# A hybrid attention block on Trainium2: a least distance between the score rows of four attention units in a build-time schedule

## The chip, the core and the metric

The kernel runs on one core of a Trainium2 chip. The metric is the time of one execution on the device, in microseconds (us). The kernel before takes 422.29 us, the median of three runs (421.83 to 422.44).

## The reference

One decoder layer with two token mixers on an input of 512 tokens and 1024 channels in fp32. Both read one normed input through one combined projection. The first mixer ("A", MoBA) has eight heads of 64 channels with block-sparse attention. The sequence has only two blocks of 256 keys and the top three are taken, so every query sees all keys before it. The second mixer ("B", NSA) has eight heads with a compressed, a selected and a window branch. Both outputs are gated, projected and merged, and go through one output projection. What matters here is the attention of mixer A:

```python
def moba_mixer(q, k, v, bias_tab):
    scale = 1.0 / math.sqrt(Dh)
    ...
    def one_chunk(c):
        ...
        logits = jnp.einsum('bhqd,bhqnkd->bhqnk', qc, kg).astype(jnp.float32) * scale
        dist = tq[:, None, None] - (sc[..., None] * MOBA_BLOCK + offs)
        bias = bias_tab[hi[..., None], t5_bucket(dist)]
        logits = jnp.where(dist >= 0, logits + bias, NEG)
        p = jax.nn.softmax(logits.reshape(B, H, Q_CHUNK, -1), axis=-1).astype(v.dtype)
        return jnp.einsum('bhqm,bhqmd->bhqd', p, vg.reshape(B, H, Q_CHUNK, -1, Dh))
...
    h = rms_norm(x, norm_w[l])
    proj = h @ w_in[l]
    ...
    k_cmp = rms_norm(compress(heads(kc), cmp_pos_k[l], cmp_w1_k[l], cmp_w2_k[l]), k_norm_cmp[l])
    ...
    merged = g_m[..., :D_MODEL] * (y_a @ w_branch_a[l]) + g_m[..., D_MODEL:] * (y_b @ w_branch_b[l])
    x = x + merged @ w_out[l]
```

## The kernel before

**Tiling.** Tokens come in four tiles of 128 rows. fp32 products are made of three passes over a high and a low part: L402 casts a weight tile to its high part on ScalarE (ACT), L412 subtracts it on VectorE (DVE) for the low part, and L437 holds the three matmuls. The projections go one group of columns after another (`ORDER`: `qk0 v kc vc qk1 za0 kb za1 za2 qb za3 vb zb0` and so on); then come the gates and branch products of both mixers and the output product, in the same stream (`gemms`).

**The attention.** A *unit* is one head of mixer A (units 0 to 7) or one head and branch of mixer B (units 8 to 23). Units 0 to 3 use the queries and keys of the group `qk0`, units 4 to 7 those of `qk1`. A unit has four *rows*, one for each 128 queries, and takes the longest first (512, 384, 256, 128 keys). For each row:

- `Unit.qk` (L1078) takes one of the two PSUM banks for scores (`room("s")`, L1085) and makes two matmuls into `sps` (L1094).
- `bias` (L1107) adds the bias table `T` and takes the row's minimum on DVE (L1114). That reads the bank out and frees it. The result goes to a buffer `sb`.
- `soft` (L1121) takes the exponential with its sum on ACT (L1125), scales by the reciprocal (L1127, L1128) to a high half in fp16 on ACT (L1132) and makes the low half on DVE (L1136).
- `send` (L1057) transposes both halves by DMA into `dst` (L245, on the SP queue).

A `Pair` takes two units; `pv` (L1157) makes their value products `O` (L1168) when all eight rows are in `dst`. Units 4 and 5 are one pair, 6 and 7 the next. The bias table of a unit is fetched by `load_bias` (L887) into one of two buffers. The outputs of mixer A are wanted by the branch products (`branch`, L1383), which come behind all projections.

**The compression** (`compress_h`, L930) runs beside: its weights `in_w` are loaded and split (`vh`, `vl`, by L402 and L412 as well), multiplied into `hps` (L940), copied to `hs` by ACT (L947) and transposed by the small product `pu` (L952).

**What sets the order.** Nothing on the chip decides an order: the program is laid out while it is built, and each engine then takes its instructions in that order. The build walks a clock `now` in ns, from costs that it is given for each kind of work. The work on TensorE (PE) comes from streams, one generator each: scores, gemms, compression, values and others. A stream that yields a number has put that much work on PE; one that yields a function waits until the function gives a time that has passed. The loop takes, among the streams that are ready by their *margin*, the one with the least share used so far:

```python
        ws = [(r, r.wait()) for r in live]
        ok = ([r for r, w in ws if w is not None and w + r.margin <= now[0]] or
              [r for r, w in sorted(((r, w) for r, w in ws if w is not None and w <= now[0]), key=lambda z: z[1])[:1]])
```

The margin of the scores is `LATE_A` = 1000, of the values `LATE_V` = 2000, of the compression `LATE_C` = 300, of the gemms `MARGIN` = 300. The work of DVE, ACT and GpSimd comes as a `Chain` of steps behind a matmul; a step is put in its engine's order when the step before it is done by the costs (`Chain.step`, L203). Loads and transposes are put in the SP queue's order in the same way (`dma`, L236; `dma_transpose`, L243). `scores` (L1339) goes through the units in order and through each unit's rows.

Of the kernel before, what the change touches and what calls it, by code (L numbers as in the profile page):

```python
# [58 lines left out]
SHARE_C = 100.0  # L59
LAG = 20000  # L60
MARGIN = 300
LATE_A = 1000
LATE_V = 2000
LATE_S = 1000
# [44 lines left out]
def hybrid_kernel(ctx: ExitStack, tc: tile.TileContext, x, x0, xT, wtok, wchan, gains, w1,  # L109
# [21 lines left out]
    now = [0.0]  # L131
# [41 lines left out]
    class Chain:  # L173


        def __init__(c, t=None, held=False):
            c.t = now[0] if t is None else t
            c.q = deque()
            c.held = held
# [370 lines left out]
    def x_rms():  # L550
        yield need("sq")
        ready = done["sq"] + XW
        yield lambda: ready
        yield room("o")
        ps = psum("o", "pss")
        for t in range(NT):
            nc.tensor.matmul(ps[:, t:t + 1], sq_sum[:, t * P:(t + 1) * P], ones, start=True, stop=True)
            yield 214
            if t < NT - 1:
                ready = now[0] + XG  # L560
                yield lambda: ready
        c = Chain(now[0] + 230)
        c.do({"D": 70}, lambda e: e.tensor_scalar(rx, ps[:, :NT], 1.0 / D, EPS, op0=ALU.mult, op1=ALU.add), ps)
        c.do({"p": 1030}, lambda e: e.tensor_tensor(rx, rx, mhalf[:, :NT], op=ALU.pow))
        c.mark("rx").call(lambda: [fn() for fn in rx_todo])
        x_diag(c)
# [188 lines left out]
    def qk_used(*keys):  # L755
        for k in keys:
            qkt[k]["uses"] -= 1
            if not qkt[k]["uses"]:
                release(qkt[k]["t"])
# [573 lines left out]
    def prepare():  # L1333
        for n, (pre, _) in enumerate(units):
            yield lambda: 0.0 if n <= begun[0] + 2 else None
            yield from pre()
            prepared.add(n)

    def scores():  # L1339
        for n, (_, u) in enumerate(units):  # L1340
            yield lambda: 0.0 if n in prepared else None
            begun[0] = n
            for b in reversed(range(NT)):
                yield from u.qk(b)
            qk_used(u.q[:2], u.ks[:2])

# [4 lines left out]
    def values():  # L1351
        for p in pairs:
            yield from p.pv()
            todo_units[0] -= 2
# [272 lines left out]
    def cmp():  # L1627
        yield from compress_h(0)
        yield from compress_h(1)


    class Run:
        def __init__(r, gen, share, margin=MARGIN):
            r.gen, r.share, r.vt, r.wait, r.live, r.margin = gen, share, 0.0, lambda: 0.0, True, margin
# [10 lines left out]
    for k in range(KT):  # L1645
        x_split(k)
        x_square(k)
    load_consts()
    now[0] = 3500.0
    A, F, C, X, B, V = Run(scores(), SHARE_A, LATE_A), Run(gemms(), SHARE_F), Run(cmp(), SHARE_C, LATE_C), Run(x_rms(), 100.0), Run(prepare(), SHARE_B), Run(  # L1650
        values(), SHARE_V, LATE_V)
    Z = Run(starts(), 100.0)
# [95 lines left out]
```

## Time and profile before

| | |
|---|---|
| median of three runs | 422.29 us |
| the profiled execution | 422.54 us |
| its span, first to last instruction | 420.5 us |
| PE busy, matmuls | 411.8 us |
| DVE busy | 356.3 us |
| ACT busy | 297.9 us |
| the DMA queue's packets | 70.5% of 16 engines' span |
| score rows of units 4 to 7, first and last | 112.96 and 149.63 us |

A profile is of one execution. Its lines give an engine, a line of the kernel, an operation and what it writes and reads by the program's names (`out<-in`). Busy time of PE is modelled, since matmuls overlap; idle time between matmuls is what counts. A wait line says who waited for whom: total us, times, longest. A timeline line has the start, the length and, in brackets, the idle time before it and what ended that. Windows give busy time in a stretch of the span. SPq is the queue that issues the DMAs.

### The profile page before, as it was taken

To read this page: it belongs to the slowest core of one execution; us is meant where nothing else is said; L and a number is where in the kernel's file an instruction comes from. 1 tells how busy PE (TensorE), PEld (TensorE's weight loads), DVE (VectorE), ACT (ScalarE), POOL (GpSimd) and SP (SyncE) were. 2 spreads that over 40 slices of the span, in tenths; PEclk is the share of its full clock that TensorE was granted. 3 is DMA by queue.
4 is the path that set the end of the run, shared out by engine and by line. 5 is a ranking of instruction groups with operands and counts; after the bars stand their busy time and mean duration, and the time that the engine had idled before them with its cause. 6 is when DMAs were issued, how large, how long until landed. Compare 5 with 4: busy or idle time off the path is not lost.

```text
span 420.5 us, 7307 instructions
## 1 busy us (share of the span) xinstructions
PE 411.8 (98%) x2235; PEld 322.0 (77%) x2235; DVE 356.3 (85%) x933; ACT 297.9 (71%) x793; POOL 35.1 (8%) x37
## 2 busy tenths in 40 slices
PE   9999998999998999999999999999999999999996
PEld 7877875778976677897766777666777888888885
DVE  5967969999899987778999997899956967698993
ACT  7996748997797988727988897898943433445620
POOL 0015100123210033200000000000000000000000
PEclk9999999999999999999999999999999999999999
DMA  8951785688969988750878778889799597251232
GB/s 278 311 190 49 129 271 140 137 183 214 264 201 232 195 163 194 218 153 12 147 168 196 150 161 200 167 195 160 145 162 348 175 374 278 79 180 44 56 143 100
DMA packets 116693, 75.30 MB, mean 179 GB/s; under 512 B 89072, under 2 KB 92016, under 8 KB 116656
## 3 DMA queue, kind: packets, MB, share of 16 engines
q1 hardware_dynamic: 116656, 74.86, 70.5%
q8 instruction: 17, 0.28, 0.3%
q14 instruction: 20, 0.16, 0.1%
HBM read 51.11 MB, written 2.75 MB: 128 GB/s over the span
## 4 chain that ended last, share of the span: by engine, by line
PE 54%; DVE 23%; DMA 9%; ACT 5%; issue 5%; SPq 1%; POOL 1%; DVEq 0%; ACTq 0%; POOLq 0%
PE pgc L437 21%; PE pbr L437 9%; PE po L437 9%; PE pgt L437 8%; DMA wr<-in_wtok 5%; DVE sb L1114 4%; DVE wl L412 4%; DVE sb L1136 4%; DMA wr<-in_w 3%; PE O L1168 3%; PE sps L1094 3%; ACT wh L402 2%; DVE vl L412 1%; SPq L238 1%; DMA T<-rtab 1%
## 5 line engine op out<-in xcount | busy, mean ns | idle before, releaser
L437 PE MATMUL pgc<-hh,wh 128*128 128x512 f32 x208 | 87.1, 419 | 0.0
L412 DVE TENSOR_TENSOR wl<-wr,wh 128x512 fp32r<-128x512 f32 (+1 forms) x112 | 73.1, 669 | 11.8 <-ACT wh L402 11.6
L437 PE MATMUL pgc<-hh,wl 128*128 128x512 f32 x208 | 81.5, 392 | 0.0
L437 PE MATMUL pgc<-hl,wh 128*128 128x512 f32 x208 | 81.2, 390 | 0.0
L402 ACT CAST wh<-wr 128x512 fp32r<-128x512 f32 (+1 forms) x111 | 64.0, 599 | 11.2 <-DMA wr<-in_wtok 5.6
L1125 ACT ACTIVATE sb<-sb,sst 128x256 f32<-128x256 f32 (+3 forms) x96 | 53.2, 554 | 10.5 <-DVE sst L1114 10.2
L437 PE MATMUL pgt<-wh,hh 128*128 128x512 f32 (+2 forms) x160 | 58.3, 364 | 0.1
L437 PE MATMUL pgt<-wl,hh 128*128 128x512 f32 (+2 forms) x160 | 56.1, 351 | 0.5 <-DVE wl L412 0.4
L437 PE MATMUL pgt<-wh,hl 128*128 128x512 f32 (+2 forms) x160 | 55.8, 349 | 0.0
L1136 DVE SCALAR_TENSOR_TENSOR sb<-sb,sst 128x256 f16<-128x256 f32 (+3 forms) x96 | 51.1, 542 | 4.2 <-ACT sb L1132 3.9
L1114 DVE CUSTOM_DVE_ANT_0 sb<-sps,T,gst 128x512 f32<-128x512 f32 (+3 forms) x96 | 51.2, 541 | 3.5 <-PE sps L1094 1.6
L1132 ACT ACTIVATE sb<-sb,sst 128x256 f16<-128x256 f32 (+3 forms) x96 | 51.4, 552 | 4.0 <-DVE sst L1128 3.7
L437 PEld LDWEIGHTS pgc<-hh,wh 128*128 128x128 f32 x208 | 39.1, 188 | 8.6 <-issue 0.3
L437 PEld LDWEIGHTS pgc<-hh,wl 128*128 128x128 f32 x208 | 39.0, 188 | 8.6
L437 PEld LDWEIGHTS pgc<-hl,wh 128*128 128x128 f32 x208 | 39.2, 189 | 6.5
L1094 PE MATMUL sps<-qkt,qkt 128*128 128x512 f16 (+3 forms) x176 | 38.2, 310 | 1.6 <-DVE sst L1114 1.4
L489 POOL TENSOR_TENSOR nr<-nss,mhalf 128x8 f32<-128x8 f32 (+1 forms) x16 | 29.0, 1819 | 109.4 <-DVE nss L488 47.9
L437 PEld LDWEIGHTS pgt<-wl,hh 128*128 128x128 f32 x160 | 30.1, 188 | 5.5 <-DVE wl L412 1.6
L437 PEld LDWEIGHTS pgt<-wh,hh 128*128 128x128 f32 x160 | 30.2, 189 | 4.3 <-DVE X L912 0.4
L437 PEld LDWEIGHTS pgt<-wh,hl 128*128 128x128 f32 x160 | 30.2, 189 | 3.4
L1094 PEld LDWEIGHTS <-qkt 128*128 128x128 f16 x176 | 11.5, 98 | 21.4 <-issue 18.5
L437 PE MATMUL pbr<-yh,wh 128*128 128x512 f32 x64 | 26.4, 413 | 0.0
(229 smaller groups left out, 746.3 us busy)
## 6 DMA issues: line engine op xcount, KB each, us to landing
wr<-in_wchan SPq DMA_DIRECT2D x52, 256.0 KB, 3.8
wr<-in_wtok SPq DMA_DIRECT2D x36, 256.0 KB, 4.0
wq<-in_wout SPq DMA_DIRECT2D x36, 256.0 KB, 3.1
T<-rtab SPq DMA_DIRECT2D x16, 256.0 KB, 4.0
wr<-in_w SPq DMA_DIRECT2D x16, 256.0 KB, 3.7
wr<-in_wbr SPq DMA_DIRECT2D x16, 256.0 KB, 3.1
xr<-in_x SPq DMA_DIRECT2D x8, 256.0 KB, 5.3
x<-in_xT SPq DMA_DIRECT2D x7, 256.0 KB, 5.8
```

The lines of the kernel that those rows point to most:

```text
L238: nc.sync.dma_start(out=dst, in_=src)
L402: e.copy(hi, raw)
L412: c.do(either(n), lambda e, hi=hi, lo=lo, raw=raw: e.tensor_sub(lo, raw, hi.bitcast(F32))).mark((w, 1, i))
L437: nc.tensor.matmul(dst, sts[i][a], mvs[i][b], start=(start and i == a == b == 0), stop=(stop and i == n - 1 and (a, b) == passes[-1]), ski ...
L489: c.do({"p": 700 + 150 * w}, lambda e: e.tensor_tensor(v(dst), v(ss), mhalf[:parts, :w], op=ALU.pow))
L1094: nc.tensor.matmul(sps[:, :n].rearrange("p (t n) -> p t n", n=P), qs, k4[:, x, j, :b + 1], start=not x, stop=bool(x))
L1114: e.tensor_tensor_reduce(z["sb"], sps[:, :L], T[:, S - L:], scale=nrunscale, scalar=3e38, op0=ALU.add, op1=ALU.min, accum_out=st[:, 0, b:b ...
L1125: c.do({"A": 279 + 0.834 * L}, lambda e: e.activation(z["sb"], z["sb"], AF.Exp, bias=st[:, 0, b:b + 1], scale=-1.0, accum_out=st[:, 1, b:b ...
L1132: e.activation(z["pp"][:, :L], z["sb"], AF.Copy, scale=s_)
L1136: c.do({"d": 59 + cd(L)}, lambda e: e.scalar_tensor_tensor(z["pp"][:, L:], z["sb"], s_, z["pp"][:, :L], op0=ALU.mult, op1=ALU.subtract))
L1168: nc.tensor.matmul(out, v[r][kb][:, vi * DH:(vi + 1) * DH], u.moving(kb, pi), start=p.first and kb == vi == pi == 0, stop=p.last and kb == ...
```

## The change

The stream of scores gets a least distance. For units 4 to 7 it remembers the earliest time of the last row, `beat`; before each row it sets `beat` to the later of the clock and the old `beat` plus 2500 ns, and waits for that time before `qk`, which then waits for its keys and a free bank as before. All other units are as they were.

```diff
+BEAT = 2500
...
+    beat = [0.0]
+
     def scores():
         for n, (_, u) in enumerate(units):
             yield lambda: 0.0 if n in prepared else None
             begun[0] = n
             for b in reversed(range(NT)):
+                if 4 <= n < 8:
+                    t = beat[0] = max(now[0], beat[0] + BEAT)
+                    yield lambda: t
                 yield from u.qk(b)
             qk_used(u.q[:2], u.ks[:2])
```

## The prediction

> **What bounds the kernel now.** I read the windows by stage first, to see which engine a stage runs on; then TensorE's waits; then the sixteen score rows that the change moves; then what lies behind TensorE's two waits.
>
> ```profile
> span 420.5 us, 7307 instructions
> ...
> 113.00:150.00 37.00, 34.75 (x199) 26.68 (x199) 35.66 (x114) 34.08 (x108) 3.56 (x4) 1.00 0.89 207
> 150.00:188.00 38.00, 37.83 (x258) 32.78 (x256) 30.23 (x77) 26.24 (x67) 9.89 (x6) 1.00 0.78 187
> 188.00:390.00 202.00, 201.71 (x1073) 151.80 (x1073) 172.50 (x452) 139.70 (x374) 0.00 (x0) 1.00 0.71 174
> ```
>
> The first line is the page's span; the others are windows: length, busy time of PE, PEld, DVE, ACT and POOL, the granted clock, the DMA engines' share. TensorE (PE) works in nearly every microsecond, at clock 1.00. Its idle time from 113 us, where the first of the paced units runs, to 390 us is 2.25 + 0.17 + 0.29 = 2.71 us. From 390 us on only the output's product and its way out are left. The order of work before 113 us is not touched, and the change adds no instruction. So 2.71 us is all that it can win, and 2.25 of them lie between 113 and 150 us, in the stretch that it re-times. There VectorE (DVE, 35.66 of 37 us) and ScalarE (ACT, 34.08) are nearly full, and the DMA engines are at 0.89; from 150 to 188 us DVE has 7.8 us idle and ACT 11.8.
>
> The two waits that make up the 2.25 us are these, with one that lies before 113 us:
>
> ```profile
> PE pu L952 <- ACT hs L947: 1.3, 1, 1.3
> PE O L1168 <- DMA dst<-sb: 0.8, 1, 0.8
> ...
> PE sps L1094 <- DVE sst L1114: 1.4, 2, 1.1
> ```
>
> The first two are TensorE's waits between 113 and 150 us, the third is from the waits of the whole run. A score row (`sps`) waited for its bank twice, for 1.4 us in all, and both times in units 0 to 3. In units 4 to 7 no row waits. What waits there is the small product `pu` of the first compression, for ScalarE's copy `hs` (L947), and the first of the value products `O` of units 4 and 5, for its transposed weights in `dst`.
>
> The rows of units 4 to 7, two matmuls each, in TensorE's timeline (start, length):
>
> ```profile
> 112.96 0.60 PE L1094 MATMUL sps<-qkt,qkt 128*128 128x512 f16 x2
> 113.88 0.50 PE L1094 MATMUL sps<-qkt,qkt 128*128 128x384 f16 x2
> 116.15 0.39 PE L1094 MATMUL sps<-qkt,qkt 128*128 128x256 f16 x2
> 117.85 0.28 PE L1094 MATMUL sps<-qkt,qkt 128*128 128x128 f16 x2
> 120.56 0.60 PE L1094 MATMUL sps<-qkt,qkt 128*128 128x512 f16 x2
> 122.17 0.50 PE L1094 MATMUL sps<-qkt,qkt 128*128 128x384 f16 x2
> 123.89 0.39 PE L1094 MATMUL sps<-qkt,qkt 128*128 128x256 f16 x2
> 125.52 0.28 PE L1094 MATMUL sps<-qkt,qkt 128*128 128x128 f16 x2
> 128.44 0.61 PE L1094 MATMUL sps<-qkt,qkt 128*128 128x512 f16 x2
> 130.73 0.50 PE L1094 MATMUL sps<-qkt,qkt 128*128 128x384 f16 x2
> 133.94 0.66 PE L952 MATMUL pu<-cst,hs 128*128 128x64 f32 x4 [1.32 <-ACT hs L947]
> 134.43 0.38 PE L1094 MATMUL sps<-qkt,qkt 128*128 128x256 f16 x2
> ...
> 136.05 0.29 PE L1094 MATMUL sps<-qkt,qkt 128*128 128x128 f16 x2
> 138.68 0.59 PE L1094 MATMUL sps<-qkt,qkt 128*128 128x512 f16 x2
> 141.87 0.50 PE L1094 MATMUL sps<-qkt,qkt 128*128 128x384 f16 x2
> 144.26 0.39 PE L1094 MATMUL sps<-qkt,qkt 128*128 128x256 f16 x2
> 147.86 1.66 PE L1168 MATMUL O<-dst,v 128*64 128x512 f16 x22 [0.79 <-DMA dst<-sb]
> 149.63 0.29 PE L1094 MATMUL sps<-qkt,qkt 128*128 128x128 f16 x2
> ```
>
> The sixteen rows take 149.63 − 112.96 = 36.7 us, 2.44 us apart in the mean, but unevenly: the first eight come in 12.6 us (1.8 us apart), the last eight in 21.2 us (3.0 apart). The row taken early does not come out early:
>
> ```profile
> 122.14 0.74 DVE L1114 CUSTOM_DVE_ANT_0 sb<-sps,T,gst 128x512 f32<-128x512 f32 x1
> ...
> 124.55 0.71 ACT L1125 ACTIVATE sb<-sb,sst 128x512 f32<-128x512 f32 x1
> 132.63 0.71 ACT L1132 ACTIVATE sb<-sb,sst 128x512 f16<-128x512 f32 x1
> ...
> 133.67 0.75 DVE L1136 SCALAR_TENSOR_TENSOR sb<-sb,sst 128x512 f16<-128x512 f32 x1
> ```
>
> These are the four long steps of the row of 120.56: 0.74 + 0.71 + 0.71 + 0.75 = 2.9 us of work, finished 13.9 us after the row (134.42). Eleven of these microseconds are spent in the queues of DVE and ACT, where the row's steps stand among the splits of the weights and the copies that the products wait for.
>
> **The change part by part.** *The distance.* The scheduler's times are not in the trace; I let the trace's times stand for them, which is a choice. A row's earliest time is the later of now and 2.5 us after the previous earliest time. The rows' stream carries a margin of 1.0 us (`LATE_A`): it is preferred only 1.0 us after the time it waits for. The first row of unit 4 has asked long before its keys have landed, so it stays at 112.96. The second asks when the first is done, some 0.4 us later, and comes 1.0 us behind that, at 114.4 (now 113.88). From there on one comes every 2.5 us: row k at 114.4 + 2.5 (k − 2). Row 8 comes at 129.4 (now 125.52), row 9 at 131.9 (128.44), row 12 at 139.4 (136.05), row 16 at 149.4 (149.63). The distance is kept while the program is laid out; on the chip there is no instruction for it and no engine waits for it. So the change takes the burst out: rows 2 to 15 move back by 0.5 to 3.9 us, and the last row stays within a few tenths. Removed from TensorE: nothing. It fills the moved places with chunks of the projections that would have come later; the sum of its work is the same.
>
> *The wait of `pu`.* Behind it stand a load, a split and a copy:
>
> ```profile
> 125.56 4.64 DMA wr<-in_w
> ...
> 130.22 0.62 ACT L402 CAST vh<-wr 128x512 fp32r<-128x512 f32 x1 [2.34 <-DMA wr<-in_w]
> ...
> 133.53 0.35 ACT L947 COPY hs<-hps 128x256 f32<-128x256 f32 x1
> ...
> 140.68 3.02 SPq L238 DMA_DIRECT2D wr<-in_wtok  x2
> 143.81 2.49 SPq L245 DMA_TRANSPOSE dst<-sb  x2
> ...
> 155.06 5.25 SPq L245 DMA_TRANSPOSE dst<-sb  x4
> ...
> 163.19 1.82 PE L1168 MATMUL O<-dst,v 128*64 128x512 f16 x24
> ```
>
> The first line is of the chain that ended last, the next two of ACT's timeline, two of the SP queue's, one more of SP's and one of TensorE's. A load of the compression's weights is issued at 125.56, when DVE has freed its buffer, and lands 4.64 us later; ACT stands still for 2.34 us until it can split it, and `hs`, which is queued behind that split, starts at 133.53, after the step of 0.71 of row 5 (132.63). TensorE has stood for 1.32 us by then. With the distance, row 6 is taken 2.2 us later, so that its step on DVE (at most the 0.74 of a full row) falls behind the split that frees the load's buffer, and the load goes out up to 0.7 sooner. Row 5 is ready 1.3 us later and row 8 by 3.9, so one or two of their steps on ACT, 0.71 each at most, fall behind `hs`. Together 0.7 + 0.7 = 1.4 to 0.7 + 1.4 = 2.1 us, more than the wait. The bounds: 1.3 us won if `hs` comes in time; nothing if the load lands when it does now; and up to 1.1 lost, because TensorE, rid of rows 9 and 10 (0.61 + 0.50), can reach `pu` that much sooner. I take 1.3 won, as both reliefs point that way and their smaller sum already covers it.
>
> *The wait of the value product.* The last two transposes of units 4 and 5 are issued at 143.81 and 1.2 us later, behind two loads that hold the SP queue from 140.68 to 143.70; the product stands 0.79 us for them. Rows 7 and 8, which feed them, are taken 3.0 and 3.9 us later. But they spend over ten microseconds in queues, so their last steps move by less, and the scheduler, which places the product by its own estimate of the landing, moves it too. Bounds: the 0.8 goes, or it grows by one more transpose ahead in the queue (5.25 / 4 = 1.3), to 2.1. I leave it at 0.8.
>
> *What else moves.* The rows' transposes go past loads in the SP queue, each 1.3 us of it; TensorE waits for no load now, so I cost that at nothing. The bias table of unit 6 can only be fetched once unit 4's last row has been read, 1.5 us later (row 4: 119.4, now 117.85); it is wanted by row 9, which moves by 3.5. The key and query buffers of units 4 to 7 are freed by their last rows; row 16 does not move, so the second mixer's queries find theirs as now. From 188 us the order may come out otherwise, since it is made step by step from what went before; there are 0.29 us of idle time to win there and I cost it at nothing.
>
> *The sum.* The profiled execution took 422.54 us, 2.0 more than its span and 0.25 more than the median of 422.29. 422.54 − 1.3 = 421.2 for it, and 422.29 − 1.3 = **421.0** against the median. The floor is 422.29 − 2.71 = 419.6.
>
> **The rivals.** *Both waits go:* 422.29 − 1.3 − 0.8 = 420.2. For it: DVE and ACT are nearly full to 150 us and have 7.8 and 11.8 us free behind, and spreading the burst relieves both. Against it: the last row does not move, and by then the same work has to be done.
>
> *Nothing that can be measured:* 422.3. The mean distance is 2.44 us already, so the change only evens out what has the same total; the load may land as late as now (4.64 us with the DMA engines at 0.89), or the 1.3 us may turn up at another product. That the distance does not bind at all speaks against the rows: nine of the fifteen intervals are under 2.5 us.
>
> *Slower: the second value product becomes late.* The transposes of units 6 and 7 decide it. Their last four leave the SP queue from 155.06 to 160.31 and the product starts at 163.19 without a wait, 2.9 us behind the last issue. In the new order rows 13 to 16 come at 141.9 to 149.4, evenly, right behind rows 9 to 12; units 6 and 7 now take 21.2 us, then 17.5 us between their first and last row. If the distance comes on top of the long intervals instead of filling them (the nine short ones raised to 2.5 give 1.58 + 0.23 + 0.80 + 0.89 + 0.78 + 0.87 + 0.21 + 0.88 + 0.11 = 6.4 us), row 16 comes at 156, and the transposes are issued until some 166. It decides from the point where the last issue is later than 160.3 by more than the scheduler has moved the product. Price: the wait of the first product, 0.8, taken a second time, and one more transpose (1.3) ahead of each: 0.8 + 2 × 1.3 = 3.4, less the 1.3 of `pu`: 422.3 + 2.1 = 424.4. For it: the first product does stand for its transposes. Against it: 2.9 us are more than any transpose's 1.3. [...]
>
> **How the numbers follow.** 0.2% of 422.29, about what a measurement of this kernel can tell from no change, is 0.84 us. The forecast (421.0, own range 420.5 to 421.4) has 0.34; both waits gone or more (420.2), 0.17: faster 0.51. Nothing that can be measured, 0.27. Slower 0.22, half of it for the value product at 424.4 and half for a smaller loss in an order that came out otherwise (the 1.1 us at `pu`, 423.4). The range begins at the floor, 419.6, as no known cost lies under it, and ends at 423.8, between the smaller loss and the value product's price; what is left out is the upper part of the slower cases, 0.1, and something under the floor, 0.05.
>
> **What would show it.** Right: the waits of TensorE between 113 and 150 us no longer name `pu` for `hs`, or for less than 0.3 us; the score rows of units 4 to 7 run 2 to 3 us apart, the second some 1.5 us behind the first, the last near 149; PE's idle time from 113 to 150 us is near 0.9; the load of 125.56 goes out sooner or lands sooner; the instruction count is 7307 as now. Wrong in its step: `pu` still waits for `hs` by more than 1 us, or another product waits in its place. Wrong altogether: a wait of `O` for `dst` at both value products of units 4 to 7 by over 1 us; rows over 3 us apart in the mean, so that the last comes after 153; or over 1 us of new idle time behind 188 us, where I expect none.

## The result and the profile after

| | before | after |
|---|---|---|
| median | 421.83 us (15 runs) | 423.70 us (15 runs, 422.51 to 425.72) |
| the profiled execution | 422.54 us | 423.71 us |
| its span | 420.5 us | 421.7 us |
| score rows of units 4 to 7, first and last | 112.96 and 149.63 us | 112.15 and 152.55 us |

Ratio after to before: 1.0052, 95% interval 1.0037 to 1.0066. One run of the kernel before took 452.72 us, in a slower state, and is left out of the ratio; the two medians give 1.0044. The change makes the kernel slower by half a per cent, where 421.0 us and a gain were forecast. In the new kernel the line numbers from the change's first line up to `scores` are one higher.

The page's first line, against 7307 before (the matmuls are 2235 in both; DVE's instructions are 933 before and 932 after, ScalarE's 793 and 794):

```profile
span 421.7 us, 7303 instructions
```

The windows of the changed kernel over the forecast's stretches (length, then busy time of PE, PEld, DVE, ACT, POOL, the granted clock, the DMA share):

```profile
113.00:150.00 37.00, 36.36 (x190) 27.50 (x191) 36.83 (x120) 34.82 (x108) 6.25 (x5) 1.00 0.92 215
150.00:188.00 38.00, 37.62 (x277) 32.33 (x274) 29.23 (x71) 24.57 (x63) 5.38 (x4) 1.00 0.73 173
188.00:390.00 202.00, 199.86 (x1055) 149.98 (x1054) 169.39 (x445) 139.57 (x373) 0.00 (x0) 0.99 0.69 174
```

TensorE's idle time from 113 to 150 us went from 2.25 to 37 − 36.36 = 0.64 us: a gain of the size that was forecast is there, and 0.3 us more. From 188 to 390 us it went from 0.29 to 202 − 199.86 = 2.14 us. All of that is one wait, by TensorE's waits from 113 us on:

```profile
PE O L1169 <- DMA dst<-sb: 2.1, 1, 2.1
PE pu L953 <- ACT hs L948: 0.6, 1, 0.6
PE hps L941 <- DVE vl L413: 0.2, 1, 0.2
PE hps L941 <- ACT vh L403: 0.2, 1, 0.2
```

It is not the product of units 4 and 5, nor of 6 and 7, but the 9th of the twelve, in the second mixer, 120 us behind the last paced row. In TensorE's timeline:

```profile
272.63 0.40 PE L1169 MATMUL O<-dst,vb 128*64 128x512 f16 x1
275.18 3.41 PE L1169 MATMUL O<-dst,vb 128*64 128x512 f16 x23 [2.14 <-DMA dst<-sb]
```

Its first matmul runs, the next waits 2.14 us, and the other 23 then take 3.41 us. The same product before:

```profile
275.89 1.82 PE L1168 MATMUL O<-dst,vb 128*64 128x512 f16 x24
```

So it also runs 3.41 − 1.82 = 1.59 us longer. The windows show why, by the granted clock (the column before the last two):

```profile
274.00:276.00 2.00, 0.82 (x4) 0.36 (x6) 1.14 (x3) 2.00 (x7) 0.00 (x0) 0.76 0.92 177
276.00:278.00 2.00, 2.00 (x20) 1.64 (x17) 0.00 (x0) 0.67 (x3) 0.00 (x0) 0.50 0.72 175
278.00:280.00 2.00, 2.00 (x11) 1.06 (x9) 0.84 (x3) 0.04 (x1) 0.00 (x0) 0.89 0.99 304
```

Idle time between 113 and 390 us is 0.64 + 0.38 + 2.14 = 3.16 us, against 2.71. With the slow product, 3.16 + 1.59 − 2.71 = 2.0 us are lost. The first paced row, before which nothing is changed, came 0.8 us earlier in this execution, so 2.0 − 0.8 = 1.2 us remain, and the two profiled times differ by 1.17. That the sum closes so well is chance: by the starts of TensorE's next entries (278.52, and 277.64 before) the product took 5.89 us from its first matmul, against 1.75, which is 0.4 us more than the wait and these 1.59 us together.

What the product waited for stands in the SP queue. Before:

```profile
267.68 6.97 SPq L245 DMA_TRANSPOSE dst<-sb  x5
274.74 0.54 SPq L238 DMA_DIRECT2D T<-rtab  x1
```

After:

```profile
265.74 3.44 SPq L246 DMA_TRANSPOSE dst<-sb  x2
269.23 0.57 SPq L239 DMA_DIRECT2D wr<-in_wchan  x1
269.91 1.17 SPq L246 DMA_TRANSPOSE dst<-sb  x1
271.13 0.57 SPq L239 DMA_DIRECT2D T<-rtab  x1
271.80 3.90 SPq L246 DMA_TRANSPOSE dst<-sb  x3
```

Before, the last four transposes of the product (by the order laid down in the build) go out one behind the other, the first four of the five from 267.68; the fifth is the next pair's. After, two go out, then a weight load, a transpose of the *next* pair and a bias table, and only at 271.80 the product's last one. Its row was finished on DVE at 267.50 + 0.64 = 268.14, as the second of the two steps in this line of DVE's timeline:

```profile
267.50 0.64 DVE L1137 SCALAR_TENSOR_TENSOR sb<-sb,sst 128x128 f16<-128x128 f32 x2
```

So it stood 3.7 us in the queue, 271.80 − 269.23 = 2.57 of them behind those three. In the kernel before, the same row was finished as the second of these two steps:

```profile
270.58 0.61 DVE L1136 SCALAR_TENSOR_TENSOR sb<-sb,sst 128x128 f16<-128x128 f32 x2
```

That is at 271.19, so after the change the row came 3.05 us sooner, and TensorE's product 275.89 − 272.63 = 3.26. In this execution the row had kept nearly all of TensorE's lead, and lost it in the queue.

Nothing of units 8 to 23 was edited. But the build lays the program out step by step, so an early shift changes later choices: of TensorE's 2689 entries the two kernels differ from entry 688 on, and only the last 428 are the same again. The order that follows some 190 us I call the *later order*; there are two main ones in what follows, that of the kernel before and that of the changed one.

### The profile page after: what moved, and what is told of

Same layout as the page of the kernel before. It is cut to its first block, busy times and chain, and to the rows that moved or that the text cites. A ratio compares the mean times of both kernels' runs of the same rounds, so it can differ in the third digit from the quotient of the medians.

```text
span 421.7 us, 7303 instructions
## 1 busy us (share of the span) xinstructions
PE 412.8 (98%) x2235; PEld 322.6 (77%) x2235; DVE 355.3 (84%) x932; ACT 298.8 (71%) x794; POOL 33.5 (8%) x37
## 4 chain that ended last, share of the span: by engine, by line
PE 77%; DVE 10%; DMA 5%; ACT 5%; issue 2%; SPq 0%; POOL 0%; DVEq 0%; POOLq 0%
PE pgc L438 25%; PE pgt L438 15%; PE pbr L438 10%; PE po L438 9%; PE pgf L700 5%; PE sps L1095 5%; PE O L1169 4%; DMA wr<-in_w 3%; DVE wl L413 2%; DVE sb L1115 2%; DMA wr<-in_wtok 2%; DVE sb L1137 1%; DVE vl L413 1%; ACT wh L403 1%; ACT vh L403 1%
## 5 line engine op out<-in xcount | busy, mean ns | idle before, releaser
L1126 ACT ACTIVATE sb<-sb,sst 128x512 f32<-128x512 f32 (+3 forms) x96 | 53.3, 556 | 11.9 <-DVE sst L1115 11.6
L1137 DVE SCALAR_TENSOR_TENSOR sb<-sb,sst 128x512 f16<-128x512 f32 (+3 forms) x96 | 51.0, 544 | 4.3 <-ACT sb L1133 4.1
L1133 ACT ACTIVATE sb<-sb,sst 128x512 f16<-128x512 f32 (+3 forms) x96 | 51.0, 553 | 4.9 <-DVE sst L1129 4.4
L490 POOL TENSOR_TENSOR nr<-nss,mhalf 128x8 f32<-128x8 f32 (+1 forms) x16 | 26.4, 1659 | 105.6 <-DVE nss L489 60.9
```

The lines of the kernel that those rows point to most:

```text
L490: c.do({"p": 700 + 150 * w}, lambda e: e.tensor_tensor(v(dst), v(ss), mhalf[:parts, :w], op=ALU.pow))
L1126: c.do({"A": 279 + 0.834 * L}, lambda e: e.activation(z["sb"], z["sb"], AF.Exp, bias=st[:, 0, b:b + 1], scale=-1.0, accum_out=st[:, 1, b:b ...
L1133: e.activation(z["pp"][:, :L], z["sb"], AF.Copy, scale=s_)
L1137: c.do({"d": 59 + cd(L)}, lambda e: e.scalar_tensor_tensor(z["pp"][:, L:], z["sb"], s_, z["pp"][:, :L], op0=ALU.mult, op1=ALU.subtract))
```

## The experiments

Five groups of kernels follow; each ratio is to the kernel before on the same chip, whose median was 421.5 to 421.9 us. The expectations name their theories; each group's question is said ahead.

**First group: is it the distance or the order behind it?** ORDER says that the place of the 9th product in the later order costs; LEAD, that TensorE comes earlier by what it won and gives that back, because the attention's steps are not earlier by as much.

Distance for units 4 and 5 alone, and for 6 and 7 alone:

```diff
-                if 4 <= n < 8:
+                if 4 <= n < 6:
```

> The distance for units 4 and 5 alone. From the second compression on, the order of all engines' work is that of the kernel before. Theory ORDER (the changed kernel loses because the later order puts the first value product of the last two heads' selected branch, the ninth in all, ahead of its transposes): the wait of pu for hs shrinks by 0.7 to 1.3 us, TensorE is some 1.5 us ahead at 190 us and stays so: 420.0 to 420.8. Theory LEAD (TensorE's lead itself is given back, since the attention's chain over DVE, ACT and the SP queue is not ahead by as much): TensorE is ahead until the ninth product and then waits there for dst by 1 to 2 us: 421.5 to 423.5, the higher end if the granted clock falls behind the wait.

Measured: 423.85 us, ratio 1.0054 (1.0023 to 1.0084). It has the later order of the kernel before (last 1568 entries the same) and is slow all the same, at a place of its own:

```profile
174.79 0.38 PE L623 MATMUL psv<-vst,onesr 128*128 128x1 f32 x2 [1.62 <-DVE vst L613]
```

Here the clock counts: behind this wait of 1.62 us the granted clock falls to 0.50 from 176 to 178 us. From 240 to 310 us nothing is lost (69.70 of 70 us busy). Its times scatter from 420.55 to 426.81; the seven runs with a mean clock of 0.996 or less have 423.56 or more, four of the five others 421.88 or less.

```diff
-                if 4 <= n < 8:
+                if 6 <= n < 8:
```

> The distance for units 6 and 7 alone. The order is that of the kernel before up to unit 6 and that of the changed kernel from the second compression on. pu keeps its wait of 1.3 us, so TensorE has no lead at 190 us. Theory ORDER: the ninth product still waits by 2 us and the clock falls behind it: 424 to 426. Theory LEAD: without the lead the ninth product comes 2 us later and waits by less than 1 us: 421.5 to 422.5.

Measured: 424.54 us, ratio 1.0075 (1.0046 to 1.0103). It has the later order of the changed kernel (last 1574 entries) and waits 1.2 us at the 9th product, with the clock at 1.00.

The changed kernel with the 9th product offered 1.5 us later to the scheduler, and with 40 matmuls of a constant put ahead of it, which add work and fill its wait:

```diff
             if p.first:
                 yield room("o")
+                if p is pairs[8]:
+                    t = now[0] + 1500
+                    yield lambda: t
```

> The changed kernel with its ninth value product alone held back in the scheduler, so that it stands some 3.5 us of work later in TensorE's order; the order before it is unchanged. Theory ORDER: its wait of 2.1 us goes, and with it the fall of the clock: 4 us less than the changed kernel, 419.5 to 420.5. Theory LEAD: the wait turns up at a later product; some 421.5 to 422.5, as the half clock behind the long wait costs 1.7 us and that is saved.

Measured: 423.25 us, ratio 1.0045 (1.0024 to 1.0067). 0.2 us of wait is left at the product, and TensorE waits at two other places:

```profile
266.20 0.50 PE L1095 MATMUL sps<-qkt,qkt 128*128 128x384 f16 x2 [1.10 <-DVE sst L1115]
...
276.12 0.59 PE L1095 MATMUL sps<-qkt,qkt 128*128 128x512 f16 x2 [1.09 <-DVE sst L1115]
```

TensorE waits at the score banks, in sum for as long (2.2 us). The first of the two waits lies ahead of the product, where the orders of both kernels are the same, so the edit can't have made it; behind the product the later order came out otherwise as well.

```diff
+            if p is pairs[8]:
+                for _ in range(40):
+                    nc.tensor.matmul(o[:, :P], ...warm..., ...warm..., start=True, stop=True)
```

> The changed kernel with 40 matmuls of 128 columns on a constant, some 2.2 us in all, put ahead of the ninth value product into its own bank, which the product then starts afresh: TensorE works where it stood idle. Every other order is unchanged. If the fall of the granted clock to a half behind the idle stretch costs 1.7 us: 422.0, with the clock at 1.00 throughout. If the clock has no part in it: no less than the changed kernel, 423.7, and up to 424.2 where the wait would have been shorter than the filling.

Measured: 424.03 us, ratio 1.0070 (1.0044 to 1.0095). No wait of O and no fall of the clock (69.43 of 70 us busy from 240 to 310 us, clock 1.00), and no gain. The changed kernel's own runs say the same of the clock: twelve of the fifteen have a mean clock of 0.999 or 1.000, and these take 422.51 to 424.83 us. So the clock's fall is not what makes the median slow. That the wait makes it is not shown by this test, but fits it: filled, it costs as much.

ORDER in this narrow form, the place of one product, falls: with the product moved its time was missed by 2.8 us, and with units 4 and 5 alone by 3; only the 424 to 426 for units 6 and 7 came true, with a shorter wait than it had and no fall of the clock. LEAD's times were missed in all three runs that it had one for, and in the changed kernel's profile the attention's row was ahead by nearly as much as TensorE.

**Second group: distance against later order.** Other distances give one later order or the other, which allows a table of two by two. TAIL: the later order costs, the spaced rows gain. HEAD: spacing costs as such.

```diff
-BEAT = 2500
+BEAT = 2400
```

> The distance set to 2400 instead of 2500. The rows of units 4 to 7 come nearly as in the changed kernel, but TensorE's order behind some 190 us comes out as in the kernel before (its last 1568 of 2689 entries are the same). Theory TAIL: the loss lies in the later order that came out with 2500, so here the gain of the head (about 1 us by 190 us) stays: 420.4 to 421.6 where the kernel before has 421.5, ratio 0.997 to 1.000, and no wait of the 9th value product over 0.5 us. Rival HEAD: spacing the rows itself costs, whatever comes later: 423.2 to 424, ratio 1.004 to 1.006, as with the distance of units 4 and 5 alone.

> The distance set to 1500, under the 1.8 us that the rows take by themselves in the burst. The first two value products of units 4 to 7 stand where the kernel before has them by TensorE's work (136.0 and 151.9 us of work), but the order behind some 190 us is that of the changed kernel (last 1615 of 2689 entries the same). TAIL: without the head's gain and with the later order's loss: 423.3 to 425, ratio 1.004 to 1.008, with waits of TensorE for O or sps of 1.5 us or more between 240 and 290 us. HEAD: as the kernel before, 421.2 to 422, ratio 0.999 to 1.001.

> The distance set to 2750, wider than in the changed kernel, with the later order of the kernel before (last 1596 of 2689 entries the same). TAIL: 420.4 to 422, ratio 0.997 to 1.001, as with 2400. HEAD: more distance costs as much or more: 423.5 to 425, ratio 1.005 or more. The value product of units 6 and 7 stands 8 us of TensorE's work later than in the kernel before; if that work behind it fails to cover the score rows, both are slower by up to 1 us.

> The changed kernel again, unaltered, beside the others on the same chip. Both theories: 423 to 424, ratio 1.003 to 1.007. If the wait of 2.1 us at the 9th value product is the order's, it is there again (1.5 to 2.5 us in O or at the score banks between 250 and 290 us); the fall of the clock to 0.50 behind it may be missing, and then the loss from 240 to 310 us is 2 us and not 4.

| distance | later order of the kernel before | later order of the changed kernel |
|---|---|---|
| none, or too small to space the rows | 1 (the kernel before) | 1500: 1.0025 (1.0009 to 1.0042), 423.05 us |
| 2400 to 2750 | 2400: 0.9988 (0.9970 to 1.0005), 421.10 us; 2750: 0.9967 (0.9947 to 0.9986), 420.55 us | 2500 again: 1.0072 (1.0048 to 1.0095), 424.58 us |

TAIL's signs hold (with 2400 there is no clear difference from the kernel before), and HEAD falls. TAIL's size is too large with 1500: 1.0025 for 1.004 or more. The same spacing is no loss or a gain with one later order and a loss with the other, and the later order costs without the spacing. With 1500, TensorE's idle time from 113 to 188 us is 2.1 us, against 2.4 in the kernel before, and from 188 to 390 us 1.3 against 0.3, so in its profile too the loss is behind 188 us. In the repeated run of the changed kernel the idle time from 113 to 188 us is 2.5 us, so the gain of the first profile is not steady. The waits from 240 to 310 us follow. With 1500, at the 9th product:

```profile
275.92 1.82 PE L1169 MATMUL O<-dst,vb 128*64 128x512 f16 x23 [1.05 <-DMA dst<-sb]
```

With 2500 again:

```profile
278.38 3.13 PE L1169 MATMUL O<-dst,vb 128*64 128x512 f16 x23 [2.37 <-DMA dst<-sb]
```

With 2750, by the window:

```profile
240.00:310.00 70.00, 70.00 (x407) 49.19 (x406) 60.90 (x187) 62.12 (x182) 0.00 (x0) 1.00 0.86 177
```

2750 is faster than both kernels; its waits from 113 to 312 us are 0.8 us in all. TAIL does not say why the two kernels of the changed order differ, 1.0025 and 1.0072: with the spacing that order costs more, not less.

**Third group: the place in the SP queue.** QUEUE: the last transpose is late because of what stands ahead of it on SP. CHAIN: DVE's and ACT's steps are late as a whole.

The changed kernel with that transpose put ahead of the three issues, no other engine's order touched (each issue is counted; issues 218 to 220 are held until 221 has gone):

```diff
+    def sp_queue(fn):
+        sent[0] += 1
+        if sent[0] in (218, 219, 220):
+            late.append(fn)
+            return
+        fn()
+        if sent[0] == 221:
+            for f in late:
+                f()
```

> The changed kernel with one place of the SP queue altered: the last transpose of the 9th value product goes ahead of the weight load, the next pair's transpose and the bias table's load that stood before it (269.23 to 271.80 in the changed kernel's profile); the orders of the other engines are those of the changed kernel to the last instruction. Theory QUEUE: these three cost the product 2.57 us in the queue, and with the transpose issued near 269.2 it lands near 272.5, when TensorE is there (272.6): the wait of 2.1 us shrinks to 0.4 or less, no clock fall behind it, and the time falls by 2 to 3 us, to 420.3 to 421.9, ratio to the kernel before 0.996 to 1.001. Rival CHAIN: the steps of the rows on DVE and ACT are as a whole behind TensorE and the lead is given back at the next product or score bank: 423 to 424.5, ratio 1.003 to 1.007.

Measured: 423.05 us, ratio 1.0030 (1.0008 to 1.0052). The 9th product runs through without a wait:

```profile
275.39 1.82 PE L1181 MATMUL O<-dst,vb 128*64 128x512 f16 x24
```

But the transpose went out at 271.86, not near 269.2, for its row was finished only then:

```profile
271.19 0.65 DVE L1149 SCALAR_TENSOR_TENSOR sb<-sb,sst 128x128 f16<-128x128 f32 x2
```

And TensorE gets there 2.8 us later than in the changed kernel's profile (0.7 of it a later start, by the first paced row at 112.86). It has waited at the score banks, and DVE, which empties them, for transposes. Waits from 188 to 312 us, of TensorE, then of DVE:

```profile
PE sps L1107 <- DVE sst L1127: 2.1, 3, 1.0
```

```profile
DVE sb L1127 <- DMA dst<-sb: 5.0, 4, 1.6
```

The three longer ones of the four waits of DVE in its timeline, in front of rows of 128 keys, which want one of four small buffers that a transpose reads last:

```profile
249.94 0.35 DVE L1127 CUSTOM_DVE_ANT_0 sb<-sps,T,gst 128x128 f32<-128x128 f32 x1 [1.53 <-DMA dst<-sb]
...
266.21 0.35 DVE L1127 CUSTOM_DVE_ANT_0 sb<-sps,T,gst 128x128 f32<-128x128 f32 x1 [1.63 <-DMA dst<-sb]
...
284.41 0.35 DVE L1127 CUSTOM_DVE_ANT_0 sb<-sps,T,gst 128x128 f32<-128x128 f32 x1 [1.44 <-DMA dst<-sb]
```

The kernel before has 0.7 us of such waits in the same stretch. The first two of these waits lie ahead of the first altered issue, at 271.86, where all orders are those of the changed kernel, whose first profile has 0.64 us of such waits. So they differ from one execution to the next. What is more of them here, 1.53 + 1.63 − 0.64, and the later start make 3.2 of the 3.7 us by which the row was late; this profile doesn't show what a row in time would have won. The time is at the low end of CHAIN's, and QUEUE's (up to 421.9) was missed.

The reverse in the kernel before: issue 219, the 9th product's last transpose, held until 222 has gone.

> The kernel before with the reverse done: the last transpose of the 9th value product goes behind the three issues that followed it (a transpose, the bias table's load, a transpose: 1.29 + 0.64 + 1.36 = 3.3 us by the profile of before); nothing else is altered. QUEUE: it is issued near 275.5 and lands near 278, 2 us or more after TensorE is there (275.9): a wait of 1.7 to 2.6 us at the 9th product, and 1.5 to 4 us more time: 423.3 to 426, ratio 1.004 to 1.010. CHAIN: one product's lateness is made good, as DVE and ACT are not moved: 421.5 to 422.5, ratio within 0.002 of 1.

Measured: 423.29 us, ratio 1.0045 (1.0027 to 1.0063), and

```profile
275.56 0.40 PE L1180 MATMUL O<-dst,vb 128*64 128x512 f16 x1
277.41 1.79 PE L1180 MATMUL O<-dst,vb 128*64 128x512 f16 x23 [1.45 <-issue]
```

The profile names no releaser here. The held transpose is the second of three that leave the SP queue from 273.67 on, 3.87 / 3 = 1.3 us each, and the product went on 2.4 us behind its issue; in the kernel before, the same transpose landed 274.53 − 272.17 = 2.36 us behind its own. Putting one transpose behind three other issues in the SP queue, with no other engine's order altered, makes a wait of 1.45 us and a loss of 0.45%, nearly that of the whole change: QUEUE's lowest time, and well over CHAIN's 421.5 to 422.5. The wait is under the 1.7 to 2.6 us expected, as the transpose was issued near 274.97 and the product went on at 277.41, 0.6 us sooner than I had the landing (278).

> The distance for units 4 and 5 alone, as before, with the norm's small product psv of the last projection (vb) offered to the scheduler half a microsecond later; the later order is that of the kernel before. QUEUE, which sees no loss in this later order: the wait of psv (1.6 us at 172.9 and the clock's fall behind it) is a place of its own, and without it the distance of units 4 and 5 is even with or better than before: 420.3 to 421.9, ratio 0.997 to 1.000, and no scatter above 424. CHAIN: pacing costs as such: 423 or more, ratio 1.004 or more. Should the wait of psv move to the next step behind it instead of going, the time stays near 423.8 by either.

```diff
+        if name == "vb":
+            t0 = now[0] + 500
+            yield lambda: t0
```

Measured: 422.30 us, ratio 1.0004 (0.9986 to 1.0023), 0.4 us above what QUEUE gave and well under CHAIN's 1.004; one run is over 424 (424.21). The wait of `psv` is gone, and 1.2 us stand at `hps` in its place. So most of the excess with units 4 and 5 was that one wait, with what the clock did behind it, and not the spacing.

**Fourth group: the loads out of SP's queue.** The 47 loads between some 190 and 315 us go to GpSimd's queue; all other orders stay.

```diff
-        nc.sync.dma_start(out=dst, in_=src)
+        (nc.gpsimd if 171 <= sent[0] < 273 else nc.sync).dma_start(out=dst, in_=src)
```

> The changed kernel, with the 47 weight and table loads that it issues between some 190 and 315 us put on GpSimd's queue, which has no work there, instead of SP's; TensorE's, VectorE's and ScalarE's orders are those of the changed kernel to the last instruction, and the transposes keep their order in SP's queue. Theory QUEUE: the loss of the later order is the time that finished rows stand in SP's queue behind loads and other rows' transposes, where they hold the buffers and the value product; with two loads of 0.65 us fewer ahead of the 9th product's last transpose and some 10 us fewer in all, the wait of O there falls from 2.1 to 0.8 us or less, DVE's waits for buffers held by transposes stay under 1 us between 188 and 310 us, and the time is 420.5 to 422.3, ratio 0.997 to 1.001. Rival ORDER OF THE STEPS: DVE and ACT work in an order that makes the rows late whatever the queue: 423 to 424.5, ratio 1.003 to 1.006.

> The same loads on GpSimd's queue, and the last transpose of the 9th product ahead of the next pair's as well. QUEUE: neither a wait of O nor of sps over 0.5 us between 240 and 310 us: 420 to 421.8, ratio 0.996 to 1.000. ORDER OF THE STEPS: about as with the transpose put ahead alone, 422.5 to 423.5, ratio 1.002 to 1.004.

> The kernel before with its loads of the same stretch on GpSimd's queue: the control, since that order loses nothing in this stretch (69.77 of 70 us busy). Both theories: no gain but what the move itself does, ratio 0.998 to 1.002; over 1.002 would mean that an issue on GpSimd costs by itself, and then the two other runs are to be read with that taken off.

> The distance of 2750, which was faster than both kernels, with the loads of the same stretch on GpSimd's queue. QUEUE: this later order has nothing left to win there, so as without it: 420 to 421.5, ratio 0.995 to 0.999. ORDER OF THE STEPS: the same. It repeats the gain of 2750 under another queue, and shows if that was chance: 421.5 to 422.5 if so.

Measured: 1.0179 (1.0140 to 1.0218), 1.0163 (1.0120 to 1.0205), 1.0070 (1.0046 to 1.0095) and 1.0098 (1.0063 to 1.0134). The control alone is 0.7% slower, and the fastest kernel lost 1.3%, so every time that was expected here was missed, and this test doesn't tell the theories apart. What it does show is in the median time from issue to landing of the transposes from 188 to 312 us, before and with its loads on GpSimd's queue:

```profile
dst<-sb SPq DMA_TRANSPOSE x63, 3.2
```

```profile
dst<-sb SPq DMA_TRANSPOSE x64, 3.7
```

With the loads on the other queue a transpose landed half a microsecond or more later after its issue (3.7 us instead of 3.2 in the kernel before, and 3.9 instead of 3.2 in the changed one). The loads landed later too (the most frequent, `wr` from `in_wchan`, after 4.5 us instead of 3.8 in the kernel before, and after 4.0 instead of 3.2 in the changed one), so which of the two makes the loss is not shown.

**Fifth group: buffers.** The four small buffers of 1.5 KB laid out in the same memory as two for rows of 256 keys and four of 0.75 KB for rows of 128, every order as it was.

```diff
+                               at=("s0", 4) if not b else ("sh", 2) if b == 1 else None)
```

> As the kernel with the 9th product's last transpose put ahead, and the four small row buffers (1.5 KB, shared by the rows of 256 and 128 keys) laid out as two of 1.5 KB for the rows of 256 keys and four of 0.75 KB for those of 128, in the same memory; every engine's order, SP's too, is that of the kernel with the transpose ahead. There VectorE stood 5.0 us in 4 waits between 188 and 310 us, all at rows of 128 keys, for a buffer whose transpose had not landed, and TensorE behind it at the score banks. Theory QUEUE: with buffers to spare these waits go (under 1 us left), the waits for sps between 240 and 310 us fall from 2.1 to 0.5 us or less, and the time is 420 to 422, ratio 0.996 to 1.001. Rival ORDER OF THE STEPS: DVE's order makes the rows late in any case: other waits of DVE and TensorE take their place, 422.5 to 424, ratio 1.002 to 1.005.

> The changed kernel with these buffers and nothing else altered (SP's order as in the changed kernel). Both theories: the 9th product still waits for its last transpose, 1.5 to 2.6 us, as nothing is moved in SP's queue, and the time is 422.5 to 424.5, ratio 1.002 to 1.007. QUEUE: no wait at the score banks of over 0.5 us between 240 and 310 us beside it.

> The kernel before with these buffers, the control: DVE waits there only 0.7 us for such buffers between 188 and 310 us and TensorE 0.3 us at the score banks, so 421 to 422.3, ratio 0.998 to 1.001 by both theories. Were the rows of 256 keys to wait for their two buffers in the first mixer, it would be slower, and the other two runs are to be read with that taken off.

Measured: 1.0051 (1.0027 to 1.0075), 1.0062 (1.0028 to 1.0097), 0.9999 (0.9981 to 1.0018). With the transpose put ahead, DVE's waits went from the rows of 128 keys to those of 256, of which there are now only two buffers:

```profile
261.28 0.48 DVE L1129 CUSTOM_DVE_ANT_0 sb<-sps,T,gst 128x256 f32<-128x256 f32 x1 [1.01 <-DMA dst<-sb]
...
283.89 0.48 DVE L1129 CUSTOM_DVE_ANT_0 sb<-sps,T,gst 128x256 f32<-128x256 f32 x1 [2.31 <-DMA dst<-sb]
```

They are 3.3 us in place of 5.0, and TensorE stands 1.67 us at a score bank behind the second. QUEUE's time was missed. The buffers are short in this order whichever rows have them, which fits late transposes, but it leaves open whether more memory would do.

**What is settled and what is not.** Shown: with all sixteen rows spaced, the loss goes with the later order and not with the spacing (second group), though spacing units 4 and 5 alone made a wait of its own ahead of that order; one transpose's place in the SP queue is enough for a loss of that size (the reverse), and in both profiles of the changed kernel the wait for that transpose is the longest that TensorE meets behind 113 us. Not shown: that this wait is the whole loss. Put ahead, the transpose leaves 0.30% (0.08 to 0.52) where the changed kernel has 0.52% (0.37 to 0.66) and 0.72% (0.48 to 0.95); these intervals overlap, so how much was won is open, while a rest of the loss is clear of zero. Not settled either: whether TensorE's waits at the score banks, behind DVE, behind transposes, make that rest, and whether they come from SP's order or from that of DVE's steps. A fifth small buffer beside the four, the direct test, was not tried.

## Why the prediction was wrong

**The distance** was right in kind: the first nine rows come 2.1 to 2.9 us apart, the second at 114.23 (114.4 forecast, met because the first came 0.8 us early: it is 2.1 us behind the first, not 1.4), the 8th at 129.95 (129.4), the 9th at 132.82 (131.9). The last came at 152.55, not 149.4: the last seven came 1.7 to 4.7 us apart.

```profile
112.15 0.60 PE L1095 MATMUL sps<-qkt,qkt 128*128 128x512 f16 x2
114.23 0.50 PE L1095 MATMUL sps<-qkt,qkt 128*128 128x384 f16 x2
...
129.95 0.29 PE L1095 MATMUL sps<-qkt,qkt 128*128 128x128 f16 x2
130.88 0.66 PE L953 MATMUL pu<-cst,hs 128*128 128x64 f32 x4 [0.64 <-ACT hs L948]
132.82 0.61 PE L1095 MATMUL sps<-qkt,qkt 128*128 128x512 f16 x2
...
149.54 1.82 PE L1169 MATMUL O<-dst,v 128*64 128x512 f16 x24
152.55 0.29 PE L1095 MATMUL sps<-qkt,qkt 128*128 128x128 f16 x2
```

**`pu`** won 0.7 of its 1.3 us, not all of it. The first relief came, larger than forecast: the load went out at 123.00, 2.6 us sooner, and its split on ACT started at 126.58, 3.6 us sooner. The second did not: row 5's step fell behind `hs`, but other steps took its place, and `hs` followed at 130.47, 3.9 us behind the split instead of 3.3. That is 3.1 us sooner than before. But TensorE stood at `pu` from 130.24 instead of 132.62, 2.4 us sooner (0.8 of it the start), where 1.1 was allowed. In the repeated run of the changed kernel it waits 1.5 us again, so that gain is not steady. **The value product** of units 4 and 5, left at 0.8 us, lost its wait (the row of 149.54 has no idle time). The two together are 1.5 of the 1.6 us from 113 to 150 us, against the 1.3 of the sum. So the sum for this stretch came out nearly right by luck: too much for `pu`, nothing for the product.

**The step that failed** is "From 188 us on the order may come out otherwise, since it is made step by step from what went before; there are 0.29 us of idle time to win there and I cost it at nothing." I priced a new order by what idle time it could remove, and not by what it could add: 2.14 us of wait at one product, and the 1.59 us that it ran longer in this execution. The prediction's own sign for this, over 1 us of new idle time behind 188 us, came true (1.85 us). The profile of before had the size of that in a window that it left out:

```profile
240.00:310.00 70.00, 69.77 (x405) 49.22 (x405) 61.43 (x192) 61.97 (x183) 0.00 (x0) 1.00 0.82 173
```

DVE and ACT are busy for 61 to 62 of 70 us, and the 9th product (275.89) started 1.4 us after its last transpose had landed (274.53). There was no idle time to win, and little to spare. The runs put the price of the other order at 0.25% without the spacing (1.1 us) and 0.5 to 0.7% with it. The same step shows in the rivals: the slower one had the right kind (a product late for its transposes) and nearly the right time (424.4), but at the product of units 6 and 7, where TensorE waited for nothing.

**The queues.** "The rows' transposes go past loads in the SP queue, each 1.3 us of it; TensorE waits for no load now, so I cost that at nothing" looked at the wrong passenger: what a load, a table and another row's transpose delay there is a transpose, and 2.57 us of them were the wait.

**The floor** of 419.6 us supposed that time won early stays won. TensorE reached the 9th product 272.63 against 275.89, 3.3 us sooner (0.8 of it the start of this execution), and stood until its transposes came.

**The clock** was in no term. The granted clock fell to 0.50 behind the 2.14 us of idle time and cost 1.59 us of the profiled execution (the product's 3.41 us against 1.82 before). The runs without such a fall, twelve of the fifteen with 422.51 to 424.83 us, show that the median hardly depends on it.

**The sign** followed from this: the forecast's own case and the two-waits case, 0.51 together, priced the first 40 us behind the change and took the other 200 as given. 423.70 lies just within the range (to 423.8), by the smaller loss that it took in. That is luck: that loss (423.4) was priced at `pu`, which waited less than before.

**A reading** was off as well: of the 1.4 us that score rows waited for a bank, 1.12 lie in units 0 to 3 (at 73.65 us) and 0.29 in the second mixer (at 240.23 us). No term of the sum uses it.

## What to carry to other kernels

In a program laid out by a list scheduler, an edit's effect ends where the order is the same again, not where the edit ends: compare the whole order before pricing the edit, and price what lies between by its slack, not by its idle time. To judge the edit itself, vary its size a little until the later order is the old one: 2500 lost half a per cent, 2400 none, and 2750 won a third of one, which is the better kernel of the study. And where an issue queue is taken in order, as SP's was here (a finished row stood 3.7 us in it, 2.57 of them behind three other issues), look at each value that ends a long chain: which transfers stand ahead of it there, and are they needed sooner?

## What the runs showed of the hardware

In these profiles the granted clock fell behind some of TensorE's idle stretches of 1.6 to 2.4 us and not behind another. It was 0.50 for some 3.4 us behind the 2.14 us of the changed kernel, by its three windows: (0.24 + 0.50 + 0.11) × 2 / 0.50. It fell as well behind 1.62 us (at `psv`, units 4 and 5 alone: 0.50 from 176 to 178 us) and 2.37 us (the changed kernel again: 0.50 from 280 to 282 us); with the buffers altered and the transpose not moved, 1.92 us passed without a fall (1.00 in each 2 us from 272 to 282):

```profile
276.27 1.82 PE L1171 MATMUL O<-dst,vb 128*64 128x512 f16 x23 [1.92 <-DMA dst<-sb]
```

That product takes its usual 1.82 us. So the length alone does not decide among these four, and in the changed kernel's profile the wait and the slow product behind it took 2.14 + 1.59 = 3.73 us together. And loads issued on GpSimd's queue were no relief to transposes: in the kernel before they landed after 3.7 us in the median instead of 3.2, in the changed one after 3.9 instead of 3.2.
